# Moving the memory rows of a cross-attention into the input stage of a decoder-block kernel

## The chip, the cores and the metric

One NeuronCore of a Trainium2 chip runs the whole program. The metric is the device time of one execution in microseconds; the median of several executions counts. The engines are named as in the profile: PE (TensorE), DVE (VectorE), ACT (ScalarE), POOL (GpSimd) and SP (SyncE, which here only issues loads and stores).

## The reference, cut to what matters

One layer of a decoder: 512 tokens of width 1024, 256 memory tokens, float32.

```python
def hybrid_layer(h, mem, ...):
    z = rmsnorm(h, norm_mix) @ w_in
    z_rw, z_dsa, z_gate = _split(z, (RW_COLS, DSA_COLS, GATE_COLS))
    y_a = rwkv7_branch(z_rw, ...)          # a recurrence over the tokens, 8 heads
    y_b = dsa_branch(z_dsa, ...)           # indexer, top-k keys, attention in a latent space
    g_a, g_b = jnp.split(jax.nn.sigmoid(z_gate + b_gate), 2, axis=-1)
    h = h + (g_a * (y_a @ w_proj_a) + g_b * (y_b @ w_proj_b)) @ w_out
    h = h + cross_attention(rmsnorm(h, norm_cross), rmsnorm(mem, norm_mem), w_cq, w_ckv, w_co)
    h = h + hier_moe(rmsnorm(h, norm_ffn), ...)
    return h

def cross_attention(hn, mem_n, w_cq, w_ckv, w_co):
    k, v = jnp.split((mem_n @ w_ckv).reshape(B, M, 2, X_HEADS, X_HEAD_DIM), 2, axis=2)
    ...
```

The memory rows depend on nothing but an input: `rmsnorm(mem, norm_mem)` and its keys and values can be computed at any time before the cross-attention.

## The kernel before, in words

The kernel is written in program order and a scheduler sets each engine's instructions in an order of its own; waits follow from the places in SBUF that instructions read and write. Places are handed out by hand: `big` (object `M`) lives throughout, and further regions live for a stage. The input stage has two, `xparts` on the right of the free space (the split input rows and split weights) and `rawring` (object `E`: raw weights and scratch). When the stage is closed (`front.close()`), the regions `memory` (object `KR`) and `early` (object `MX`) are laid over them, and what is written there waits until the input stage is done with the bytes below. `memory` lies over `xparts` alone, `early` over both.

To keep float32 precision, a matrix product is made of three passes over a high and a low part. A helper (line 197, `split`) makes the parts: ACT casts the high part, DVE or POOL subtracts for the low one. `Ring.load` (line 223) loads a weight block on SP's queue and splits it; the ring's raw places and parts are reused in turn.

The stages, in the order of time:

- Input stage (to line 789). 38 blocks of `w_in`, each 24 products of line 230. The last 16 blocks are gates (lines 587 to 591): ACT takes a Tanh, POOL's queue stores the tile to DRAM. Odd gates have their low parts on POOL, even ones on DVE. Between these products runs the recurrence in 8 chunks (lines 699 to 744; the copy of line 719 and the one of line 744 are links of its chain), the group norm (lines 750 to 759, with two squares buffers `sq`), and the indexer (lines 482 to 507): scores through two buffers `rels`, then 16 pairs of a maximum (line 501) and a replacement (line 502) on DVE for each of three query tiles. The inverse of line 625 uses scratch of `E` and gives it back.
- Attention and memory stage (lines 792 to 854). `keys_values` is a generator: it normalises the memory rows (`mem_norm`, line 564: loads at 567 and 569, square at 191, root at 176, scaling at 193), transposes them (line 810), splits them into `mT`, and makes keys (line 821, 192 products of 256 columns) and values (line 832, 96 products of 512). Keys and values are stored to DRAM (lines 824, 838). `attend` (line 510) does one query tile of the sparse attention: latent queries (517), scores (524), exponential (528), transposes (537), sums (545). The scheduler sets products of line 821 between those of `attend`.
- Mixing (lines 857 to 896): both branches are lifted by `w_pa` and `w_pb` (line 887), gated and summed; the residual rows `h` are loaded from `x` (line 871). Then the output projection, the cross-attention, the router and the experts, which the change doesn't touch.

SP issues its loads in one order; one that waits holds up those behind it.

Of the kernel before, what the change touches and what calls it, by code (L numbers as in the profile page):

```python
# [13 lines left out]
T, D, P = 512, 1024, 128  # L14
NT = T // P
# [72 lines left out]
def build(tc, I, out):  # L88
    nc = tc.nc
    V, S, G, PE = nc.vector, nc.scalar, nc.gpsimd, nc.tensor  # L90
# [14 lines left out]
    M = Mem(pool.tile([P, NBIG], F32, name="big"), NBIG)  # L105

    def region(stack, name, n, dt, side=None):
        return Mem(stack.enter_context(tc.tile_pool(name=name, bufs=1, side=side)).tile([P, n], dt, name=name), n)
# [5 lines left out]
    def psum(tag="mm"):  # L114

        i = turn.get(tag, 0)
        turn[tag] = i + 1
        return PS[:, banks[tag][i % len(banks[tag])], :]
# [69 lines left out]
    def norm_tile(dst, src, gain):  # L188

        ss, rs = scr(1), scr(1)  # L190
        S.activation(dst, src, AF.Square, accum_out=ss)
        rsqrt(rs, ss, 1.0 / D, EPS)
        V.scalar_tensor_tensor(dst, src, rs, gain, op0=OP.mult, op1=OP.mult)

    def split(hi, lo, src, eng=None):

        return S.copy(hi, src).ins, (eng or V).tensor_tensor(lo, src, hi.bitcast(F32), op=OP.subtract).ins  # L197

    def split_half(hi, lo, src):

        S.activation(hi, src, AF.Copy, scale=0.5)
        V.scalar_tensor_tensor(lo, src, 0.5, hi.bitcast(F32), op0=OP.mult, op1=OP.subtract)
# [33 lines left out]
    E = region(front, "rawring", NX + NK - NR1, F32)  # L236
# [71 lines left out]
    omm = M.get(14)  # L308
# [8 lines left out]
    hb = M.get(16)  # L317
    cb = M.get(P)
    pc = M.get(4, NCH)
    msk = M.get(2, 64)  # L320
    zxg = M.get(T)
    cw = M.get(NT, 132)
    cT = M.get(T)
    zv = M.get(4, T)
    AR = M.get(4, NCH, 2, 64)
    ZV = M.get(NCH, 512)
    ST = M.get(4, NCH, 256)
    AA = M.get(4, NCH, 2, 64)
# [233 lines left out]
        yield  # L562

    def mem_norm():
        nm, raw, gm_ = MX.get(2, D), MX.get(2, D), MX.get(D)
        gmem = gm_[:, :]
        nc.sync.dma_start(gmem, I["norm_mem"].partition_broadcast(P))
        for i in range(2):
            nc.sync.dma_start(raw[:, i, :], I["mem"][i * P:(i + 1) * P, :])
        for i in range(2):  # L570
            norm_tile(nm[:, i, :], raw[:, i, :], gmem)
        raw.done()
        gm_.done()
        return nm

    def chained(*gens):
# [108 lines left out]
    gst = [E.get(T) for _ in range(2)]  # L685
    isc_ = {qt: M.get((qt + 1) * P) for qt in range(1, NT)}
    inverse()
    rels, m8s = [E.get(T) for _ in range(2)], [E.get(16, 8) for _ in range(3)]
    g2 = M.get(4 * P)
    nc.sync.dma_start(g2[:, :], I["g2"])  # L690

    St = [M.get(4, 64) for _ in range(2)]
    Sp = M.get(4, 64)
    Xs = [M.get(256) for _ in range(2)]
# [50 lines left out]


    gm, gv = M.get(NCH * 4), M.get(NCH * 4)
    sq = [M.get(2, 4, 64) for _ in range(2)]
    by_head = lambda ap: ap.rearrange("p (c a) -> p c a", a=4)
    for b in range(4):  # L750
        Yb = Ys[:, b * 2:b * 2 + 2, :].rearrange("p c (a i) -> p c a i", i=64)
# [32 lines left out]
    pace(bg, [lambda i=i: gate(i) for i in range(16)], 3)  # L784
    for _ in bg:
        pass
    for x in (hb, *gst, *rels, *m8s, omm):
        x.done()
    front.close()

# [3 lines left out]
    MX = region(early, "early", NX, F32)  # L794
# [6 lines left out]
    ringm = Ring([MX.get(512) for _ in range(4)], [KR.get(2, 512) for _ in range(2)])  # L801
    kst, vst = [MX.get(NMEM) for _ in range(2)], [MX.get(512) for _ in range(2)]

    def keys_values():
        nm = mem_norm()
        for k in range(0, KD, 2):
            pt = psum("at")
            for j in range(2):
                for i in range(2):
                    PE.transpose(pt[:, (j * 2 + i) * P:(j * 2 + i + 1) * P], nm[:, i, (k + j) * P:(k + j + 1) * P], ident)  # L810
            split(mT[:, 0, k:k + 2, :].rearrange("p a t -> p (a t)"), mT[:, 1, k:k + 2, :].rearrange("p a t -> p (a t)"),
                  pt[:, :])
        nm.done()
        yield
        for nb in range(8):
            pt = psum()
            for k4 in range(0, KD, 4):
                w = ringm.load(I["w_ck"][nb, :, k4 * P:(k4 + 4) * P], V if k4 else G)
                for a, b in ((0, 0), (0, 1), (1, 0)):
                    for k in range(4):  # L820
                        PE.matmul(pt[:, 0:NMEM], w[:, a, k * P:(k + 1) * P], mT[:, b, k4 + k, :],
                                  start=(a + b + k4 + k == 0), stop=(a == 1 and k4 + k == KD - 1))
            S.copy(kst[nb % 2][:, :], pt[:, 0:NMEM])
            nc.gpsimd.dma_start(kT_d[:, nb, :], kst[nb % 2][:, :])
            yield
        for half in range(2):
            pts = [psum(), psum()]
            for k in range(KD):
                w = ringm.load(I["w_cv"][half, k // 2, :, k % 2 * 512:k % 2 * 512 + 512], V if k % 2 else G)
                for a, b in ((0, 0), (1, 0), (0, 1)):  # L830
                    for t in range(2):
                        PE.matmul(pts[t][:, :], mT[:, a, k, t * P:(t + 1) * P], w[:, b, :], start=(a + b + k == 0),
                                  stop=(b == 1 and k == KD - 1))
                if k % 2:
                    yield
            for t in range(2):
                S.copy(vst[t][:, :], pts[t][:, :])
                nc.gpsimd.dma_start(vm_d[:, t, half * 512:half * 512 + 512], vst[t][:, :])

    kv = keys_values()  # L840
    next(kv)

# [7 lines left out]
            pass  # L850
    for _ in kv:
        pass
    for x in (St[0], St[1], Sp, *Xs, *sq, AR, ZV, ST, AA, zxg, g2, msk, pc, cw, cT, cb, *isc_.values()):
        x.done()


# [10 lines left out]
    raws = M.get(4 * D)  # L867
    ring2 = Ring([raws[:, i * D:i * D + D] for i in (1, 2, 3, 0)], [MR.get(2, D) for _ in range(3)])
    h = M.get(NT, D)
    for i in range(NT):  # L870
        nc.sync.dma_start(h[:, i, :], I["x"][i * P:(i + 1) * P, :])
    mix = M.get(KD, T)
    gts = [M.get(2, T) for _ in range(2)]
    for x, (src, wsrc) in enumerate(((yaT, I["w_pa"]), (ybT, I["w_pb"]))):
        for k in range(4):
            split(act[:, x, 0, k, :], act[:, x, 1, k, :], src[:, k, :])
        for j in range(4):
            w = ring2.load(wsrc[j])
            gt = gts[j % 2]
            nc.gpsimd.dma_start(gt.ap, gate_d[x, j])  # L880
            for n in range(2):
                nb = j * 2 + n
                pt = psum()
                for a, b in ((0, 0), (0, 1), (1, 0)):
                    for k in range(4):
                        o = (n * 4 + k) * P
                        PE.matmul(pt[:, :], w[:, a, o:o + P], act[:, x, b, k, :], start=(a + b + k == 0), stop=(a == 1 and k == 3))  # L887

                if x == 0:
                    V.scalar_tensor_tensor(mix[:, nb, :], gt[:, n, :], 1.0, pt[:, :], op0=OP.add, op1=OP.mult)  # L890
                else:
                    V.scalar_tensor_tensor(gt[:, n, :], gt[:, n, :], 1.0, pt[:, :], op0=OP.add, op1=OP.mult)
                    V.tensor_add(mix[:, nb, :], mix[:, nb, :], gt[:, n, :])
                    if nb < 4:
                        split_half(act[:, 0, 0, nb, :], act[:, 0, 1, nb, :], mix[:, nb, :])
# [691 lines left out]
```

## Time and profile before

| | us |
|---|---|
| median of 3 runs | 1287.48 |
| lowest and highest | 1281.45, 1292.67 |
| the profiled execution | 1291.4 |
| its span | 1289.6 |
| PE, DVE, ACT, POOL busy in the span | 1196.5, 642.5, 364.9, 121.9 |

The span begins with the first instruction and ends with the last; the time of an execution also holds what lies around it. A busy engine need not be at its peak: a product counts as busy until its modelled end. Times in the rows are from the span's start. "DMA to landing" is from the issue of a transfer to its completion.

### The profile page before, as it was taken

To read this page: it belongs to the slowest core of one execution; us is meant where nothing else is said; L and a number is where in the kernel's file an instruction comes from. 1 tells how busy PE (TensorE), PEld (TensorE's weight loads), DVE (VectorE), ACT (ScalarE), POOL (GpSimd) and SP (SyncE) were. 2 spreads that over 40 slices of the span, in tenths; PEclk is the share of its full clock that TensorE was granted. 3 is DMA by queue.
4 is the path that set the end of the run, shared out by engine and by line. 5 is a ranking of instruction groups with operands and counts; after the bars stand their busy time and mean duration, and the time that the engine had idled before them with its cause. 6 is when DMAs were issued, how large, how long until landed. Compare 5 with 4: busy or idle time off the path is not lost. (4 is left out here: it accounts for less than half of the span.)

```text
span 1289.6 us, 18892 instructions
## 1 busy us (share of the span) xinstructions
PE 1196.5 (93%) x7630; PEld 865.1 (67%) x7630; DVE 642.5 (50%) x1417; ACT 364.9 (28%) x666; POOL 121.9 (9%) x110
## 2 busy tenths in 40 slices
PE   5999998999993999699999989999899999999995
PEld 5867676776672878588787777654666656565662
DVE  5246688685593654366545364424333333333325
ACT  3542322334232644522445352101010101011113
POOL 1111221111130203400000020000000000000001
PEclk7989898999796999799999998999899999999998
DMA  4311113116333213474322506999699999999891
GB/s 159 98 50 34 57 57 99 43 50 238 120 115 133 70 34 109 149 260 131 131 84 84 196 34 242 421 398 421 263 421 420 420 419 421 421 421 420 357 375 66
DMA packets 52138, 272.07 MB, mean 211 GB/s; under 512 B 6064, under 2 KB 6208, under 8 KB 27728
## 3 DMA queue, kind: packets, MB, share of 16 engines
q1 hardware_dynamic: 48544, 259.21, 52.0%
q0 software_dynamic: 3504, 11.62, 2.6%
q8 instruction: 61, 1.00, 0.3%
q14 instruction: 29, 0.24, 0.1%
HBM read 261.37 MB, written 9.44 MB: 210 GB/s over the span
## 5 line engine op out<-in xcount | busy, mean ns | idle before, releaser
L230 PE MATMUL banks<-xparts 128*128 128x512 f32 x864 | 229.3, 416 | 0.5 <-DVE xparts L197 0.5
L230 PEld LDWEIGHTS banks<-xparts 128*128 128x128 f32 x864 | 166.0, 198 | 42.2 <-issue 4.5
L1443 PE MATMUL banks<-big 128*64 128x256 f32 x1616 | 180.2, 380 | 0.0
L1443 PEld LDWEIGHTS banks<-big 128*64 128x64 f32 x1616 | 116.8, 137 | 62.2 <-issue 7.8
L230 PE MATMUL banks<-weights,rounded 128*128 128x512 f32 x384 | 93.4, 396 | 0.0
L1471 PE MATMUL banks<-big 128*64 128x512 f32 x384 | 86.6, 595 | 4.6 <-DVE big L1461 2.3
L1364 DVE TENSOR_TENSOR big<-big,banks 128x512 f32<-128x512 f32 x128 | 79.4, 681 | 5.2 <-PE banks L1362 5.2
L230 PEld LDWEIGHTS banks<-weights,rounded 128*128 128x128 f32 x384 | 70.9, 188 | 14.7 <-issue 1.0
L1448 ACT ACTIVATE slot<-banks 128x256 f32<-128x256 f32 x32 | 12.3, 385 | 222.8 <-PE banks L1460 112.2
L1412 PE MATMUL banks<-chosen,rounded 128*128 128x256 f32 x512 | 69.0, 298 | 6.6 <-DVE chosen L1166 6.3
L197 ACT CAST xparts<-rawring 128x1024 fp32r<-128x1024 f32 x38 | 39.8, 1048 | 123.5 <-PE banks L230 60.8
L1412 PEld LDWEIGHTS banks<-chosen,rounded 128*128 128x128 f32 x512 | 67.1, 206 | 8.9 <-DVE chosen L1166 6.5
L1356 DVE SCALAR_TENSOR_TENSOR chosen<-banks,big,chosen 128x512 fp32r<-128x512 f32 x32 | 24.0, 750 | 87.3 <-ACT chosen L1355 87.3
L197 DVE TENSOR_TENSOR weights<-big,weights 128x1024 fp32r<-128x1024 f32 x32 | 39.0, 1223 | 53.6 <-ACT weights L197 51.3
L1362 PE MATMUL banks<-chosen 128*128 128x512 f32 x256 | 65.6, 400 | 0.0
L1471 PEld LDWEIGHTS banks<-big 128*64 128x64 f32 x384 | 27.4, 137 | 55.6 <-issue 47.4
L197 POOL TENSOR_TENSOR xparts<-rawring,xparts 128x1024 fp32r<-128x1024 f32 x20 | 48.4, 2420 | 161.0 <-ACT xparts L197 153.3
L1355 ACT ACTIVATE chosen<-banks,big 128x512 fp32r<-128x512 f32 x32 | 22.0, 688 | 137.8 <-PE banks L1471 125.9
L1428 DVE TENSOR_SCALAR chosen<-banks,big 128x512 fp32r<-128x512 f32 x16 | 12.0, 751 | 93.7 <-PE banks L1426 93.7
L197 ACT CAST weights<-big 128x1024 fp32r<-128x1024 f32 x32 | 33.5, 1052 | 80.6 <-PE banks L230 37.8
L1362 PEld LDWEIGHTS banks<-chosen 128*128 128x128 f32 x256 | 46.1, 188 | 13.4 <-DVE big L1364 2.0
L887 PE MATMUL banks<-rounded,weights 128*128 128x512 f32 x192 | 46.7, 408 | 7.5 <-ACT weights L197 7.5
(400 smaller groups left out, 1786.9 us busy)
## 6 DMA issues: line engine op xcount, KB each, us to landing
big<-in_w_e_gate SPq DMA_DIRECT2D x51, 1024.0 KB, 13.6
big<-in_w_e_up SPq DMA_DIRECT2D x50, 1024.0 KB, 13.8
big<-in_w_e_down SPq DMA_DIRECT2D x48, 1024.0 KB, 12.2
rawring<-in_w_in SPq DMA_DIRECT2D x38, 512.0 KB, 3.6
slots<-in_w_e_up SPq DMA_DIRECT2D x14, 1024.0 KB, 14.7
slots<-in_w_e_gate SPq DMA_DIRECT2D x13, 1024.0 KB, 11.5
slots<-in_w_e_down SPq DMA_DIRECT2D x12, 1024.0 KB, 11.4
big<-in_x SPq DMA_DIRECT2D x8, 512.0 KB, 5.2
```

Source lines behind the costliest of these rows:

```text
L197: return S.copy(hi, src).ins, (eng or V).tensor_tensor(lo, src, hi.bitcast(F32), op=OP.subtract).ins
L230: r = PE.matmul(pt, st(a), mv(b), start=(first and i == 0), stop=(last and i == 2))
L887: PE.matmul(pt[:, :], w[:, a, o:o + P], act[:, x, b, k, :], start=(a + b + k == 0), stop=(a == 1 and k == 3))
L1355: r = S.activation(YE[:, 0, nh, :], pd, AF.Copy, scale=g[:, :])
L1356: V.scalar_tensor_tensor(YE[:, 1, nh, :], pd, g[:, :], YE[:, 0, nh, :].bitcast(F32), op0=OP.mult, op1=OP.subtract)
L1362: PE.matmul(pc_[:, :], PT[:, t * P:(t + 1) * P], YE[:, x, nh, :], start=(x == 0), stop=(x == 1))
L1364: V.tensor_add(hh, hh, pc_[:, :])
L1412: PE.matmul(pt[:, 0:256], HL(x, t)[:, k // 4, k % 4, :], Pr_[:, t].rearrange("p e s -> p (e s)"), start=(t == 0 and x == 0), stop=(t == NT ...
L1428: V.tensor_scalar(PT[:, :], pa[:, :], slot_id[:, :], None, op0=OP.is_equal)
L1443: PE.matmul(pu[x][hf * 64:hf * 64 + 64, :], xgs[h4][:, k % 4, es_], w[:, k % 4, hf * 256:hf * 256 + 256], start=(k == 0), stop=(k == KD - 1))
L1448: S.activation(hd_[:, :], pu[0], AF.Silu)
L1471: PE.matmul(pd[j * 64:j * 64 + 64, :], ht[:, j, fb * 2 + hf, :], w[hf][j][:, fb, nh * 512:nh * 512 + 512], start=(kb == 0), stop=(kb == 3))
```

## The change

It has four edits. `mem_norm` takes its places from the input stage: the raw rows from `E` (scratch that the inverse gave back), the gain from the two `rels` buffers, which are now one place, and the normed rows from `M`. It is called before `front.close()`, so that the scheduler can set it among the input stage's work. To make room in `M`, the two squares buffers of the group norm move into the first halves of two of the four blocks of `AR`, which the recurrence reads in its first four chunks. All splits of the value weights have their low part on DVE, where every other one was on POOL. The four loads of the residual rows move from ahead of the mixing stage to behind the loads of `w_pb`.

```diff
     def mem_norm():
-        nm, raw, gm_ = MX.get(2, D), MX.get(2, D), MX.get(D)
-        gmem = gm_[:, :]
+        nm, raw = M.get(2, D), E.get(2, D)
+        gmem = rels_[:, :]
         nc.sync.dma_start(gmem, I["norm_mem"].partition_broadcast(P))
...
         raw.done()
-        gm_.done()
         return nm
...
-    rels, m8s = [E.get(T) for _ in range(2)], [E.get(16, 8) for _ in range(3)]
+    rels_ = E.get(2 * T)
+    rels, m8s = [rels_[:, i * T:i * T + T] for i in range(2)], [E.get(16, 8) for _ in range(3)]
...
-    sq = [M.get(2, 4, 64) for _ in range(2)]
+    sq = [AR[:, i].rearrange("p c x t -> p (c x t)")[:, 0:512].rearrange("p (c a i) -> p c a i", c=2, a=4) for i in range(2)]
...
-    for x in (hb, *gst, *rels, *m8s, omm):
+    nm = mem_norm()
+    for x in (hb, *gst, rels_, *m8s, omm):
         x.done()
     front.close()
...
     def keys_values():
-        nm = mem_norm()
...
-                w = ringm.load(I["w_cv"][half, k // 2, :, k % 2 * 512:k % 2 * 512 + 512], V if k % 2 else G)
+                w = ringm.load(I["w_cv"][half, k // 2, :, k % 2 * 512:k % 2 * 512 + 512], V)
...
     h = M.get(NT, D)
-    for i in range(NT):
-        nc.sync.dma_start(h[:, i, :], I["x"][i * P:(i + 1) * P, :])
...
             w = ring2.load(wsrc[j])
+            if x == 1:
+                nc.sync.dma_start(h[:, j, :], I["x"][j * P:(j + 1) * P, :])
```

On SP, the loads from the middle of the recurrence to the opening of the next stage stood so before (`in_mem` and `in_norm_mem` are the memory rows and their gain, `in_x` the residual rows, `rawring` the input stage's region, `early` the next one's):

```order
L871 DMA big<-in_x 128x1024
L223 DMA rawring<-in_w_in 128x1024 x2
L799 DMA big<-q_d 128x512
L223 DMA rawring<-in_w_in 128x1024
L799 DMA big<-q_d 128x512 x2
L223 DMA rawring<-in_w_in 128x1024
L796 DMA early<-in_w_uk 128x512
L797 DMA early<-in_w_uv 128x512
L567 DMA early<-in_norm_mem 128x1024
L569 DMA early<-in_mem 128x1024 x2
L223 DMA early<-in_w_ck 128x512 x16
```

and from the same place of the changed program on (its lines are shifted by one to seven):

```order
L878 DMA big<-in_x 128x1024
L223 DMA rawring<-in_w_in 128x1024 x2
L800 DMA big<-q_d 128x512
L223 DMA rawring<-in_w_in 128x1024
L800 DMA big<-q_d 128x512
L567 DMA rawring<-in_norm_mem 128x1024
L800 DMA big<-q_d 128x512
L223 DMA rawring<-in_w_in 128x1024
L797 DMA early<-in_w_uk 128x512
L798 DMA early<-in_w_uv 128x512
L223 DMA early<-in_w_ck 128x512 x16
```

The gain's load has moved ahead of the last two loads of the input stage; the two loads of the memory rows stand 15 rows further ahead, between loads of `w_in`, right behind the inverse; the first load of `w_ck` has none of them before it any more. The residual rows have kept their place.

On DVE, at the beginning of the indexer's last query tile, there stood the split for gate 12 (line 197) behind four maxima:

```order
L495 SCALAR_TENSOR_TENSOR big<-rawring,big 128x512 x3
L501 MAX rawring<-big 128x8
L502 MATCH_REPLACE big<-rawring,big 128x512
L501 MAX rawring<-big 128x8
L502 MATCH_REPLACE big<-rawring,big 128x512
L501 MAX rawring<-big 128x8
L502 MATCH_REPLACE big<-rawring,big 128x512
L501 MAX rawring<-big 128x8
L197 TENSOR_TENSOR xparts<-rawring,xparts 128x1024
```

and now both scalings of the memory rows (line 193) stand around it:

```order
L495 SCALAR_TENSOR_TENSOR big<-rawring,big 128x512 x3
L501 MAX rawring<-big 128x8
L502 MATCH_REPLACE big<-rawring,big 128x512
L501 MAX rawring<-big 128x8
L502 MATCH_REPLACE big<-rawring,big 128x512
L501 MAX rawring<-big 128x8
L193 SCALAR_TENSOR_TENSOR big<-rawring,big 128x1024
L502 MATCH_REPLACE big<-rawring,big 128x512
L197 TENSOR_TENSOR xparts<-rawring,xparts 128x1024
L501 MAX rawring<-big 128x8
L193 SCALAR_TENSOR_TENSOR big<-rawring,big 128x1024
```

The first scaling waits for the gain's load, which waits for the last of the three steps of line 495; the split for gate 12 stands behind it. The split for gate 14 follows five pairs later; it has moved ahead by one pair.

On PE, the end of the last query tile and the beginning of the values were

```order
L537 MATMUL banks<-big,early 128x128 x4
L821 MATMUL banks<-memory 128x256 x6
L545 MATMUL banks<-early,big 128x128 x4
L821 MATMUL banks<-memory 128x256 x8
L559 MATMUL banks<-early 64x128 x4
L821 MATMUL banks<-memory 128x256 x31
L832 MATMUL banks<-memory 128x512 x96
```

and are

```order
L537 MATMUL banks<-big,early 128x128 x4
L821 MATMUL banks<-memory 128x256 x6
L545 MATMUL banks<-early,big 128x128 x4
L821 MATMUL banks<-memory 128x256 x8
L559 MATMUL banks<-early 64x128 x4
L821 MATMUL banks<-memory 128x256 x57
L832 MATMUL banks<-memory 128x512 x96
```

so 26 more of the 192 key products come after attention. At its beginning, the 16 transposes of line 810 stand together right behind the 144 last products of line 230. On ACT, one square of the memory rows (line 191) now stands ahead of the first copy of line 719, and the other among the steps after the recurrence; each is followed by a table load for the root, and the next Tanh by another. On SP's queue one of the four loads of `w_pa` stands behind three of the residual rows.

## Rows read from the trace of the kernel before

**Rows 1.** Busy time by stretch: us, busy (instructions) per engine, PEclk, DMA share, GB/s

```profile
core 0: us, PE busy (x) PEld busy (x) DVE busy (x) ACT busy (x) POOL busy (x), PEclk, DMA share, GB/s
...
335.00:340.00 5.00, 5.00 (x18) 3.64 (x18) 0.35 (x1) 1.43 (x2) 0.00 (x0) 0.50 0.80 289
...
416.00:418.00 2.00, 2.00 (x11) 2.00 (x11) 0.68 (x2) 1.19 (x3) 0.00 (x0) 0.50 0.03 8
...
418.00:420.00 2.00, 2.00 (x16) 1.87 (x16) 1.39 (x4) 1.15 (x2) 0.00 (x0) 0.83 0.00 0
...
420.00:422.00 2.00, 1.87 (x20) 1.68 (x19) 0.81 (x3) 1.15 (x2) 0.00 (x0) 1.00 0.01 4
...
470.00:500.00 30.00, 30.00 (x206) 22.95 (x204) 18.29 (x50) 13.67 (x32) 3.12 (x4) 1.00 0.11 36
```

**Rows 2.** Time line, all engines, 370 to 425: start us, us, engine line op, count [idle before <-releaser]

```profile
397.06 0.33 SPq L796 DMA_DIRECT2D early<-in_w_uk  x1
...
406.68 1.06 ACT L191 ACTIVATE early<-early 128x1024 f32<-128x1024 f32 x1 [12.69 <-DMA early<-in_mem]
...
414.43 1.28 DVE L193 SCALAR_TENSOR_TENSOR early<-early,big 128x1024 f32<-128x1024 f32 x1
...
415.76 2.18 PE L810 MATMUL banks<-big,early 128*128 128x128 f32 x9 [2.79 <-DVE early L193]
...
419.41 1.71 PE L517 MATMUL banks<-big,early 64*128 64x128 f32 x16
...
421.26 0.49 PE L524 MATMUL banks<-big,early 128*128 128x128 f32 x2
...
422.70 1.28 ACT L528 ACT_TABLE_LOAD   x1
...
424.00 0.41 ACT L528 ACTIVATE early<-early,big 128x128 f32<-128x128 f32 x1
```

**Rows 3.** Time line of PE alone, 318 to 395

```profile
359.94 33.28 PE L230 MATMUL banks<-xparts 128*128 128x512 f32 x144
```

**Rows 4.** Time line of DVE, 330 to 385

```profile
361.60 2.45 DVE L495 SCALAR_TENSOR_TENSOR big<-rawring,big 128x512 f32<-128x512 f32 x3
...
367.49 0.69 DVE L501 MAX8 rawring<-big 128x8 f32<-128x512 f32 x1
...
369.62 1.21 DVE L197 TENSOR_TENSOR xparts<-rawring,xparts 128x1024 fp32r<-128x1024 f32 x1
...
381.24 1.21 DVE L197 TENSOR_TENSOR xparts<-rawring,xparts 128x1024 fp32r<-128x1024 f32 x1
```

**Rows 5.** Time line of ACT in the first chunk of the recurrence

```profile
235.23 0.58 ACT L668 COPY big<-banks 32x512 f32<-32x512 f32 x1 [9.86 <-PE banks L662]
...
240.99 0.37 ACT L719 COPY big<-banks 64x256 f32<-64x256 f32 x1
```

**Rows 6.** DMA issues: line, queue, op, count, KB each, median us to landing

```profile
early<-in_mem SPq DMA_DIRECT2D x2, 512.0 KB, 8.6
...
early<-in_norm_mem SPq DMA_DIRECT2D x1, 512.0 KB, 7.3
...
big<-in_norm_cross SPq DMA_DIRECT2D x1, 512.0 KB, 4.8
...
early<-in_w_uk SPq DMA_DIRECT2D x1, 256.0 KB, 2.6
```

**Rows 7.** Key and value products in the time line; then groups of the splits: busy us, mean ns

```profile
503.92 3.97 PE L821 MATMUL banks<-memory 128*128 128x256 f32 x31
...
507.73 9.82 PE L832 MATMUL banks<-memory 128*128 128x512 f32 x42
...
520.11 2.11 PE L832 MATMUL banks<-memory 128*128 128x512 f32 x6 [2.56 <-ACT memory L197]
...
L197 POOL TENSOR_TENSOR memory<-early,memory 128x512 fp32r<-128x512 f32 x16 | 21.6, 1350 | 54.9 <-ACT memory L197 48.0 <-ACT big L561 6.8
...
L197 DVE TENSOR_TENSOR memory<-early,memory 128x512 fp32r<-128x512 f32 x16 | 12.3, 768 | 27.0 <-ACT memory L197 21.9 <-PE banks L821 3.6 <-PE banks L832 1.5
```

More of the change, by code (lines that the diff above doesn't have):

```diff
@@ L852, in build @@
         pass
-    for x in (St[0], St[1], Sp, *Xs, *sq, AR, ZV, ST, AA, zxg, g2, msk, pc, cw, cT, cb, *isc_.values()):
+    for x in (St[0], St[1], Sp, *Xs, AR, ZV, ST, AA, zxg, g2, msk, pc, cw, cT, cb, *isc_.values()):
         x.done()
```

## The prediction

> **What bounds the kernel now.** I read the busy times by stretch first, because one share over the whole span hides the stages. They show TensorE (PE) busy nearly everywhere: in the middle of the attention stage it has work in 30.00 of 30.00 us [rows 1]. So work moved from one place to another is worth nothing unless it ends idle time of PE. I then looked for a hole, and the time line of all engines has one [rows 2, 3]. The last product of the input stage ends at 359.94 + 33.28 = 393.22 us. The loads for the next stage are issued only at 397.06 us, when the last gate tile has been stored and the region that held it is free. Then a chain runs with nothing beside it: the memory rows land, ScalarE (ACT) squares them at 406.68, VectorE (DVE) scales the second tile at 414.43, PE transposes at 415.76, and attention proper begins with line 517 at 419.41. That is 26 us in which PE does almost nothing, and its clock drops with it: granted 0.50 (the 1.2 GHz level) at 416 to 418 us, back to 1.00 (2.4 GHz) after 420 [rows 1]. This hole is the only stretch of such length that the change touches. Behind it PE is full again, so what is won here should arrive at the end.
>
> **The change part by part.** All of it is reckoned against the profiled execution (1291.4 us, of which 1289.6 are span).
>
> First part, memory rows. Their two loads and the load of the gain now go to the input stage's own region, so nothing of the normalisation waits for 397.06 any more. What ends the hole then? PE finishes the input stage; 397.06 - 393.22 = 3.84 us later the weights w_uk are requested, as before (the gate store is unchanged); they land 2.6 us after issue [rows 6]; then line 517 runs. The transposes of line 810 need only the normed rows and fit into these 6.4 us (16 of them; before, nine took 2.18 us [rows 2]). So with F for the end of the input stage, line 517 starts at F + 6.4 and the first scores of line 524 another 421.26 - 419.41 = 1.85 us later.
>
> Now F, which pays for the move at two places.
> (a) ACT takes a square of 1.06 us [rows 2] ahead of the copy of line 719 that ran at 240.99 us without a wait [rows 5]. That copy is a link of the first chunk of the recurrence. The memory rows must have landed by then. Their loads can go when the inverse's last products (line 662) are done, at 235.23 us [rows 5]. Landing is the open price: two loads took 8.6 us beside three others [rows 6], and a broadcast of 512 KB with less beside it took 4.8. I take 5, the nearer row, since little else is in flight; then ACT does not wait and the link is 1.1 us late, and PE has four more products of line 230 in that place (4 x 0.231 us, from 33.28 / 144) to fill it. Cost 0.5 us; bounds 0 and 3.7 (landing 8.6, so that the square ends at 245 and the link 4.6 us late, less the 0.9 of the four products).
> (b) The gain row is loaded into the buffer that the indexer's last step reads, and that step ends at 361.60 + 2.45 = 364.05 us [rows 4]. DVE's first scaling stands three steps behind it, at 367.49 + 0.69 = 368.2, and blocks DVE until the gain lands. With 4.8 us as a lower and 7.3 as an upper row [rows 6] it lands between 368.9 and 371.4; I take 5.3, 369.4, as one load of a weight block is beside it. The scaling takes 1.28 [rows 2], the split of a gate weight 1.21, and a step of the indexer 0.75 (14 of them fill the time from 370.83 to 381.24 [rows 4]): ready at 369.4 + 1.28 + 0.75 + 1.21 = 372.6 instead of 370.8. Gate 12 begins at 359.94 + 2 x 5.55 = 371.0 and needs that split in its third product, at 371.5: PE waits 1.1 to 1.2. Behind it stand one step, the second scaling and eleven steps before the split for gate 14, 12 x 0.75 + 1.28 + 1.21: ready at 384.1 instead of 382.45. Gate 14 needs it at 371.5 + 1.1 + 11.1 = 383.7; PE waits another 0.5. Cost 1.7 us; bounds 1.2 and 3.7. On SP the gain's load stands ahead of two others which wait for later events anyway.
> So F = 393.22 + 2.2 = 395.4, line 517 at 401.8, line 524 at 403.7. PE is idle for some 4 us before and the clock may have dropped; before, it came back between 2 and 4 us after PE had become dense at 415.76 [rows 1, 2], so I add 0.5: 404.2. Against 421.26 that is 17.0 us earlier.
>
> From this comes off: six products of line 821 that were done before 419.41 and must be done later, 6 x 0.128 = 0.8 (3.97 / 31 [rows 7]). Also, the new order leaves 57 of these products for the tail behind attention, where 31 stood. If PE is the limit of attention, this costs nothing; if the chain over DVE and ACT is, all 26 x 0.128 = 3.3 come on top. PE shows no idle time there, but weight loading is busy only 22.95 of 30 us [rows 1], so some of its busy time is waiting in disguise: I take 1.2. On the other side, ACT's table load before the first exponential, 1.28 us at 422.70 [rows 2], falls away because the tables for Tanh still stand; PE had products of line 821 under it, so 0.3 of its 0 to 1.3.
>
> ACT changes tables four times more in the input stage and twice less behind it. By the row one load takes 1.28 us, and the exponential starts 0.02 us after its end [rows 2]; ACT has idle time there, so the sum takes nothing beyond (a). The Trainium skill (ScalarE: Activation LUTs, "Table sets: the hidden batching unit") speaks against this: do all calls of one set before switching. The same page puts a switch at 2.66 us with a drain; by that the two switches more would cost 5.3 us if ACT were the limit, and the sum would be 10.4. The row shows no drain.
>
> Second part, the value weights. Eight splits go from GpSimd (1350 ns) to DVE (768 ns) [rows 7]. In the first seven steps PE took 9.82 / 42 = 0.234 us a product, without a wait; so the splits hide behind PE in either place. The one stall, 2.56 us before 520.11 [rows 7], waits for a weight load that queues on SP behind the load of the stored keys, and that order is unchanged. I take 0.4 us gained; bounds 0 and 2.6 (the stall goes).
>
> Third part, the residual rows. In the program's order their four loads stand where they stood, in the input stage, since their room comes free long before; one load of w_pa moves between them. All are needed 200 us later: 0. The squares of the group norm now lie in AR: they wait for half the recurrence, and the order puts them later; PE has products to run: 0, bounds -1 and 1.
>
> **Sum:** 17.0 - 0.8 - 1.2 + 0.3 + 0.4 = 15.7 us earlier: 1291.4 becomes 1275.7. The profiled execution lies 3.9 us above the median of the three timed runs, 1287.48; on that scale I predict 1271.8. About 1% (12.9 us) is what a measurement of this kernel can tell from no change.
>
> **Rivals.**
> Slow landings: the moved loads take as long as their rows of before, 8.6 and 7.3 us. For it: they now meet the w_in stream. Against: only one or two others are in flight, where five were. Then (a) costs 3.7 and (b) 3.7, 5.2 more: gain 10.5, 1277.0, within 1%.
> More than the sum: the key products and the denser start keep the clock at 1.00, and the value stage loses its stall (2.56): 15.7 + 0.5 + 2.6 - 0.4 = 18.4, 1269.1. Against it: the stalled load's place in the queue is the same.
> Slower: the clock. Attention would begin out of a sparse stretch, without the dense transposes and key products that brought the clock back at 418 [rows 1]. At 335 to 340 us PE is busy in 5.00 of 5.00 us and is granted 0.50 all the same, so being busy is not enough. At half clock a PE-bound us loses half a us; so this eats the gain when it lasts 32 us, and if it lasts through three of the four query tiles, some 60 us, it loses 30: 1287.5 - 15.7 + 30 = 1301.8. Against it: before, with products of the same kind, attention ran at 1.00. The Trainium skill (TensorE: Matmul & The Clock Gate, Part 1) calls the throttled state the default that activity releases; by that the clock would come back soon after 402, and the row at 335 to 340 shows a busy PE without it.
> The change does not do what it says: a wait on the region stays in the chain, and the hole moves at most by the mem loads' 2 us: 1285.5. Against it: the new order names the input stage's buffer as their target, and the splits of line 197 need only the weight half of that region.
>
> **How the numbers follow.** Forecast 0.50, slow landings 0.25, more 0.12, slower 0.07, not as said 0.06. The forecast's own range is 1268 to 1276, from its bounds; a tenth of it lies within 1%. So faster by over 1% has 0.45 + 0.12 = 0.57, slower by over 1% 0.07, and within 1% 0.05 + 0.25 + 0.06 = 0.36. The range runs from 1263, which is the second rival less the half of what the three timed runs differ, to 1284, which takes in the slow landings and leaves out the last two.
>
> **What would show it.** Right: line 517 about 17 us earlier, PE idle before it of 4 to 5 us instead of 26, line 810 directly behind the last product of line 230, DVE waiting for the gain's DMA near 368, and every later stage shifted by the same amount. Wrong: DVE or ACT waiting long for the memory or gain rows with PE idle before 395; a tail of line 821 that stands alone at the end of an attention stage no shorter than before; a granted clock of 0.5 beyond 410; or the same stage starts as now.

## The result and the profile after

| | before | after |
|---|---|---|
| median, us | 1288.88 (6 runs) | 1272.76 (6 runs) |
| lowest and highest | 1281.45, 1292.67 | 1269.44, 1276.07 |
| profiled execution, its span | 1291.4, 1289.6 | 1271.04, 1269.3 |
| PE, DVE, ACT, POOL busy | 1196.5, 642.5, 364.9, 121.9 | 1191.2, 646.6, 367.4, 111.9 |

The ratio is 0.9879, with a 95% interval of 0.9857 to 0.9902: 16.1 us less, between 12.6 and 18.4. The forecast was 1271.8.

The time line of the changed kernel where [rows 2 to 4] stood (columns as there; DVE and PE of the end of the input stage, then the start of attention):

```profile
356.99 0.33 SPq L567 DMA_DIRECT2D rawring<-in_norm_mem  x1
...
362.95 1.28 DVE L193 SCALAR_TENSOR_TENSOR big<-rawring,big 128x1024 f32<-128x1024 f32 x1 [1.85 <-DMA rawring<-in_norm_mem]
...
364.81 1.21 DVE L197 TENSOR_TENSOR xparts<-rawring,xparts 128x1024 fp32r<-128x1024 f32 x1
...
365.03 3.27 POOL L197 TENSOR_TENSOR xparts<-rawring,xparts 128x1024 fp32r<-128x1024 f32 x1 [4.13 <-ACT xparts L197]
...
366.08 11.17 PE L230 MATMUL banks<-xparts 128*128 128x512 f32 x48 [1.59 <-DVE xparts L197]
366.55 2.83 DVE L193 SCALAR_TENSOR_TENSOR big<-rawring,big 128x1024 f32<-128x1024 f32 x1
...
378.83 10.74 PE L230 MATMUL banks<-xparts 128*128 128x512 f32 x46 [1.57 <-DVE xparts L197]
...
389.41 1.47 PE L810 MATMUL banks<-big 128*128 128x128 f32 x12
...
393.39 0.33 SPq L797 DMA_DIRECT2D early<-in_w_uk  x1
...
396.23 3.06 PE L517 MATMUL banks<-big,early 64*128 64x128 f32 x16 [3.98 <-DMA early<-in_w_uk]
...
399.23 0.79 PE L524 MATMUL banks<-big,early 128*128 128x128 f32 x2
...
400.39 0.40 ACT L528 ACTIVATE early<-early,big 128x128 f32<-128x128 f32 x1 [0.46 <-DVE big L527]
```

The hole has closed: the last product of line 230 ends at 389.57, the transposes of line 810 follow at once, and what PE then waits for is w_uk alone, requested at 393.39. From the last product to the first score (line 524) it is 9.66 us; before it was 421.26 - 393.22 = 28.04 [rows 2, 3]. But the 144 products that ran without a gap now wait twice, 1.59 and 1.57 us, for a split on DVE. The first wait is the gain's landing with a scaling behind it: DVE begins the scaling at 362.95, and the split for gate 12 is ready at 366.02. In front of the second stands the other scaling, which took 2.83 us instead of 1.28. And the first exponential needs no table load.

The same stretches as in [rows 1], columns as there:

```profile
395.00:400.00 5.00, 3.77 (x19) 3.58 (x20) 0.00 (x0) 1.62 (x3) 0.45 (x1) 0.50 0.88 295
400.00:405.00 5.00, 5.00 (x26) 4.95 (x25) 3.40 (x14) 2.55 (x8) 1.93 (x2) 0.51 0.32 105
405.00:410.00 5.00, 5.00 (x41) 4.57 (x40) 4.03 (x19) 3.38 (x13) 0.74 (x2) 1.00 0.18 52
```

The granted clock still falls to 0.50 in the short gap, and is back at 1.00 after 405. The 16 products of line 517 took 3.06 us where they had 1.71 [rows 2].

PE at the end of attention, where [rows 7] stood:

```profile
481.02 0.66 PE L559 MATMUL banks<-early 128*64 128x128 f32 x8
481.61 7.10 PE L821 MATMUL banks<-memory 128*128 128x256 f32 x57
488.54 9.79 PE L832 MATMUL banks<-memory 128*128 128x512 f32 x42
500.15 2.70 PE L832 MATMUL banks<-memory 128*128 128x512 f32 x6 [1.82 <-ACT memory L197]
503.19 11.48 PE L832 MATMUL banks<-memory 128*128 128x512 f32 x48 [0.34 <-ACT early L837]
```

From the last product of line 559 to the first value product it is now 6.9 us, with 57 key products that stand alone; with 31 it was 3.7. The stall of the value stage is still there, 1.82 us.

### The profile page after: what moved, and what is told of

Read it like the earlier page. It is cut to its first block, busy times and chain, and to the rows that moved or that the text cites. A ratio compares the mean times of both kernels' runs of the same rounds, so it can differ in the third digit from the quotient of the medians.

```text
span 1269.3 us, 18889 instructions
## 1 busy us (share of the span) xinstructions
PE 1191.2 (94%) x7630; PEld 864.5 (68%) x7630; DVE 646.6 (51%) x1425; ACT 367.4 (29%) x668; POOL 111.9 (9%) x102
## 5 line engine op out<-in xcount | busy, mean ns | idle before, releaser
L1461 DVE COPY big<-banks 128x512 f32<-128x512 f32 x16 | 11.0, 690 | 84.1 <-PE banks L1460 84.1
```

## The experiments

Each is compared with runs of the kernel before on the same chip: the ratios are against these, with their 95% intervals. Their medians were 1288.94 us beside runs 1 to 4, 1287.17 beside 5 to 8 and 1286.12 beside 9 to 12; the changed kernel was measured once, where the kernel before had 1288.88. So medians of different sets compare to some 3 us only, and smaller steps are read from the stages. Each run has one profile, so a stage is one execution's. The stages below are read from the PE time line of each run's profile: "front" from the first product of gate 12 to the last of line 230, "start" from there to the first score, "attention" from the first score to the last product of line 559, "tail" from there to the first value product (negative where that one comes before the end of attention), "values" from the first to the last product of line 832.

| us | median | front | start | attention | tail | values |
|---|---|---|---|---|---|---|
| before | 1288.88 | 22.3 | 28.0 | 82.7 | 3.7 | 26.9 |
| changed | 1272.76 | 25.7 | 9.7 | 82.5 | 6.9 | 26.1 |
| 1 memory rows alone | 1276.49 | 28.9 | 9.7 | 82.5 | 6.9 | 26.9 |
| 2 the rest alone | 1284.30 | 22.3 | 27.3 | 82.7 | 3.7 | 26.3 |
| 3 scalings late | 1267.86 | 22.3 | 9.6 | 82.3 | 6.9 | 25.0 |
| 4 w_uk early | 1268.35 | 27.8 | 4.5 | 83.8 | 7.0 | 26.3 |
| 5 both | 1263.83 | 22.3 | 4.8 | 82.2 | 6.4 | 27.7 |
| 6 keys behind attention | 1285.78 | 25.7 | 9.6 | 85.8 | 23.1 | 25.3 |
| 7 keys paced | 1270.44 | 28.9 | 9.5 | 89.3 | -5.3 | 26.7 |
| 8 squares alone | 1285.35 | 22.3 | 28.3 | 82.7 | 3.7 | 27.1 |
| 9 before again | 1288.60 | 22.3 | 27.7 | 82.7 | 3.7 | 26.0 |
| 10 keys' load late | 1269.74 | 25.6 | 9.8 | 82.5 | 6.9 | 23.1 |
| 11 all four | 1255.65 | 22.3 | 4.8 | 87.8 | -5.3 | 26.8 |
| 12 three | 1258.28 | 22.3 | 4.8 | 82.0 | 6.4 | 23.3 |

**1 and 2: the parts.** Run 1 is the changed kernel with the value splits and the residual loads as before (those two parts of the diff undone). The squares of the group norm stay in `AR` in both runs, since the memory rows need their room.

> The changed kernel with the value weights split on both engines again and the residual rows loaded where they were. Theory A (the memory rows do it): about 1273.5 us, the changed kernel's time within its scatter; only the value stage (96 products of line 832) takes 26.9 us instead of 26.1. Theory B (5 to 7 us come out of the input stage from the other edits): 1278 us or more.

Run 2 is the complement, with the residual loads moved as in the change:

```diff
-    sq = [M.get(2, 4, 64) for _ in range(2)]
+    sq = [AR[:, i].rearrange("p c x t -> p (c x t)")[:, 0:512].rearrange("p (c a i) -> p c a i", c=2, a=4) for i in range(2)]
...
-                w = ringm.load(I["w_cv"][half, k // 2, :, k % 2 * 512:k % 2 * 512 + 512], V if k % 2 else G)
+                w = ringm.load(I["w_cv"][half, k // 2, :, k % 2 * 512:k % 2 * 512 + 512], V)
```

> The kernel before with all edits but the memory rows: value splits on VectorE, residual rows with the second branch, squares of the group norm in AR. Theory A: 1288 us, that is 0 to 1 us less than before; hole of 26 us between the last product of line 230 and line 517 as before; value stage near 26.1 us. Theory B: 1282 us, with the recurrence or what lies around it some 5 us shorter than before.

Run 1: 0.9910 (0.9875 to 0.9944), run 2: 0.9972 (0.9951 to 0.9992). So the memory rows bring most of it, but run 1 is 3.0 us slower than expected, with a front 3.2 us longer than the changed kernel's, and run 2 gained 3.6 (1.0 to 6.3) where theory A had 0 to 1. The first has a cause that the trace shows. DVE and POOL in run 1, columns as before:

```profile
365.77 1.29 DVE L193 SCALAR_TENSOR_TENSOR big<-rawring,big 128x1024 f32<-128x1024 f32 x1 [2.10 <-DMA rawring<-in_norm_mem]
...
367.58 2.33 POOL L197 TENSOR_TENSOR xparts<-rawring,xparts 128x1024 fp32r<-128x1024 f32 x1 [4.13 <-ACT xparts L197]
367.63 3.37 DVE L197 TENSOR_TENSOR xparts<-rawring,xparts 128x1024 fp32r<-128x1024 f32 x1
...
371.06 24.23 PE L230 MATMUL banks<-xparts 128*128 128x512 f32 x94 [4.01 <-DVE xparts L197]
```

The split for gate 12 takes 3.37 us on DVE instead of 1.21 [rows 4]: it began 0.05 us after POOL's split for gate 13, and ended 1.09 us after that one's end. In the changed kernel's profile DVE was first by 0.22 us; then POOL's took 3.27 us instead of 2.33, and it was the scaling behind it that took 2.83 us instead of 1.28. One order on each engine, two outcomes: one PE wait of 4.01 us (and a clock that falls behind it, front 28.9), or two of 1.6. Which one comes hangs on when the gain lands. In all six profiles with the scalings at this place POOL's split begins 1.15 us after gate 12's first product. Where the first scaling began 0.85 to 1.00 us before that product (the changed kernel, runs 6 and 10), DVE's split was first; where it began 0.21 to 0.66 us before it (runs 1, 4 and 7), POOL's was. In the kernel before, the two were 2.5 us apart [rows 4]:

```profile
372.11 2.42 POOL L197 TENSOR_TENSOR xparts<-rawring,xparts 128x1024 fp32r<-128x1024 f32 x1 [4.13 <-ACT xparts L197]
```

**3: the scalings behind the indexer.** `last[3]` is the indexer's final instruction, `behind` orders after it:

```diff
-        V.scalar_tensor_tensor(dst, src, rs, gain, op0=OP.mult, op1=OP.mult)
+        with behind(*after): V.scalar_tensor_tensor(dst, src, rs, gain, op0=OP.mult, op1=OP.mult)
...
-            norm_tile(nm[:, i, :], raw[:, i, :], gmem)
+            norm_tile(nm[:, i, :], raw[:, i, :], gmem, last[3])
```

> The changed kernel with both scalings of the memory rows behind the last step of the indexer, so that neither the gain's landing nor the scalings stand ahead of the splits for gates 12 and 14. Theory A (these two waits of 1.59 and 1.57 us cost their full length): the waits go, the 24 products of each gate run without a gap, 1269.5 us. Rival C (what is won there is lost in front of the first scores, since the transposes of line 810 become late): line 517 at the same distance of 6.7 us or more from the last product of line 230 plus the delay, 1272 to 1274 us.

PE of run 3:

```profile
355.22 33.32 PE L230 MATMUL banks<-xparts 128*128 128x512 f32 x144
388.38 0.27 PE L810 MATMUL banks<-big 128*128 128x128 f32 x1
388.87 1.42 PE L810 MATMUL banks<-big 128*128 128x128 f32 x11 [0.23 <-DVE big L193]
390.87 0.66 PE L810 MATMUL banks<-big 128*128 128x128 f32 x4 [0.57 <-DVE memory L197]
395.14 3.06 PE L517 MATMUL banks<-big,early 64*128 64x128 f32 x16 [3.62 <-DMA early<-in_w_uk]
```

The 144 products run without a gap again, as in [rows 3]; the transposes still end before w_uk lands. 0.9843 (0.9808 to 0.9878). Theory A holds: the front's 3.4 us are the price of the scalings' place. That they went through at the end at no cost is shown too (start 9.6 us, as in the changed kernel), so rival C falls.

**4 and 5: w_uk and w_uv early.**

```diff
-    wuk, wuv = MX.get(512), MX.get(512)
+    wuk, wuv = [AR[:, 2].rearrange("p c x t -> p (c x t)")[:, i * 512:i * 512 + 512] for i in range(2)]
```

> The changed kernel with w_uk and w_uv loaded into a block of AR that the recurrence has left, so that line 517 needn't wait for the input stage's region. Theory A (the hole that is left, 9.7 us from the last product of line 230 to the first score, is the wait for w_uk and its landing): line 517 directly behind the transposes, the first score 4.5 to 5.5 us behind the last product (the copy of line 519 still waits for the region), 1268.5 us. Rival D (half clock or a later wait eats it, since the next weights of line 821 still come with the region): the attention stage longer by what its start gained, 1271 to 1273 us.

PE of run 4:

```profile
394.04 1.47 PE L810 MATMUL banks<-big 128*128 128x128 f32 x12
396.23 0.66 PE L810 MATMUL banks<-big 128*128 128x128 f32 x4 [0.72 <-DVE memory L197]
396.83 1.75 PE L517 MATMUL banks<-big 64*128 64x128 f32 x16
398.67 1.37 PE L524 MATMUL banks<-big,early 128*128 128x128 f32 x6
```

Start 4.5 us, as expected, and line 517 at the full clock's 1.75 us. 0.9841 (0.9805 to 0.9877). Attention gave 1.3 back, while the clock was granted at 0.69 between 400 and 405 us; the front of this profile is the bad one with a wait of 4.01.

> The changed kernel with both edits at once: scalings behind the indexer, and w_uk and w_uv early in AR. Theory A (two separate costs): the gains of the two runs before, 4.9 and 4.4 us against the changed kernel's median, add up: 1263.5 us. Rival (the late scalings now stand in front of line 517, since nothing else holds it): line 517 some 2 us later behind the last product of line 230 than in the run with the early weights alone, 1265 to 1266 us.

Run 5: 0.9800 (0.9774 to 0.9826). Against the kernel before of its own set it is 23.3 us faster, where runs 3 and 4 have 21.1 and 20.6 and the changed kernel 16.1; so the two costs add up within the noise. The start is 4.8 us against 4.5 in run 4, so the late scalings do not stand in front of line 517 for the 2 us of the rival. The granted clock does not fall at all at the start of attention, which is back at 82.2.

**6 and 7: is attention full?** Run 6 holds every key product behind the last one of line 559 (`fin`); run 7 writes them between attention's steps.

```diff
-                        PE.matmul(pt[:, 0:NMEM], w[:, a, k * P:(k + 1) * P], mT[:, b, k4 + k, :],
+                        with behind(*fin): PE.matmul(pt[:, 0:NMEM], w[:, a, k * P:(k + 1) * P], mT[:, b, k4 + k, :],
```

```diff
-        for _ in attend(qt):
-            pass
+        for n, _ in enumerate(attend(qt)):
+            if (qt * 9 + n) % 4 == 3: next(kv, None)
```

> The changed kernel with all 192 key products (line 821) held behind the last product of attention, so that line 524 to line 559 run with nothing set between them. Theory A (attention is bound by its chain over VectorE and ScalarE, and the key products ride along): from the first score to the last product of line 559 it stays at 78 to 82.5 us, as with 135 products in it (82.45); then 192 products alone take 23.5 us, and the whole is 14 to 17 us slower than the changed kernel. Rival (TensorE is the bound there, as its busy share says): the stretch falls by 135 x 0.123 = 16.6 us to 66 us, and the whole is the changed kernel's time within 3 us.

PE of run 6, the first scores and the end of attention:

```profile
395.79 0.79 PE L524 MATMUL banks<-big,early 128*128 128x128 f32 x2
...
478.94 1.16 PE L545 MATMUL banks<-early,big 128*128 128x128 f32 x8 [0.68 <-ACT early L539]
480.88 0.66 PE L559 MATMUL banks<-early 128*64 128x128 f32 x8 [0.78 <-DVE early L548]
481.46 23.29 PE L821 MATMUL banks<-memory 128*128 128x256 f32 x192
```

Attention alone takes 85.8 us, no less than with 135 products set into it. Its clock is at half for 23.6 of them, 18 more than in the changed kernel's profile; had these cost their whole half, 9 us, 77 would be left, and still not 66. The last two query tiles settle it, since the clock stands at 1.00 there in both (the changed kernel first, then run 6; columns as in [rows 1]):

```profile
434.20:481.70 47.50, 46.73 (x314) 36.66 (x314) 27.88 (x78) 22.04 (x53) 5.60 (x7) 1.00 0.14 42
...
435.10:481.50 46.40, 39.90 (x249) 27.64 (x249) 25.94 (x76) 18.23 (x45) 1.11 (x2) 1.00 0.04 14
```

The 58 key products in the first of these stretches, 7 us of work, cost 1.1 us. This one execution is 13.0 us slower than the changed kernel's median. So a good part of TensorE's busy time in attention (30.00 of 30 us [rows 1]) is waiting in disguise: these key products ride along in a chain over PE, DVE and ACT that lasts nearly as long without them.

> The changed kernel with the key products written between the steps of attention (a group of 24 after every fourth step), so that none is left behind it. Theory A (attention has room): the tail of 57 products and 6.9 us goes, attention gets at most 2 us longer, 1267 to 1268 us. Rival (TensorE is full): attention grows by as much as the tail shrinks, 1272 to 1273 us.

0.9849 (0.9823 to 0.9874), which is neither theory's number. All 192 key products and 7 value products now lie inside, and attention is 6.8 us longer; from the first score to the end of the values it is 110.7 us instead of 115.4. Together the runs give the room: with 0, 135 and 155 key products (the last is the kernel before, 192 - 31 - 6) attention takes the same 82 to 86 us; the 37 keys and 7 values beyond 155 cost about their own time, 37 x 0.128 + 7 x 0.234 = 6.4. Whether it is their number or the even placement that costs this, no run separates.

**8 and 9: the input stage.** Run 8 is the kernel before with the first line of run 2's diff alone, run 9 the kernel before unchanged.

> The kernel before with one edit of the change alone: the two squares buffers of the group norm in AR. TensorE's order is that of the run with all edits but the memory rows. Theory E (that run's gain of 3.6 us is this edit's: it lets the scheduler set the recurrence's last chunks and the transposes behind it in another order, and the clock falls for a shorter time between 290 and 345 us): 1285 us, 3 to 4 us less than before, with 10 us at half clock between 280 and 350 us where there were 20. Rival F (the gain was scatter, or came from the value splits): 1288 to 1289 us.

> The kernel before, unchanged, for a second profile of it. Theory G (the 7 us by which gate 12 began earlier in the changed kernel's profile are mostly the clock's scatter between two executions): from the end of the inverse to gate 12 it takes 125.6 us plus half the time at half clock, as in the other profiles, and the time at half clock there differs from the 20.5 us of the first profile. Rival E (the order with the squares in AR spares it): again 17 to 21 us at half clock between 280 and 350 us, where the profiles with the squares in AR have 10 to 14.

Run 8: 0.9986 (0.9967 to 1.0004), unclear; the kernel before against itself: 1.0012 (0.9984 to 1.0041). Busy time by stretch of the first profile of the kernel before, and then of its second:

```profile
280.00:350.00 70.00, 69.49 (x427) 49.48 (x426) 42.01 (x108) 23.23 (x33) 10.07 (x9) 0.85 0.43 151
```

```profile
280.00:350.00 70.00, 69.47 (x433) 49.34 (x433) 45.89 (x110) 24.97 (x35) 10.61 (x10) 0.93 0.50 172
```

PE of the second:

```profile
353.72 33.29 PE L230 MATMUL banks<-xparts 128*128 128x512 f32 x144
```

The same program is granted 0.85 in one execution and 0.93 in another, with PE busy in both; that is some 5 us of full clock, (0.93 - 0.85) x 70, and its last 144 products begin at 353.72 instead of 359.94 [rows 3]. So theory G holds: the 7 us by which gate 12 came earlier in the changed kernel's profile can be scatter, since the unchanged kernel moved by 6.2. In the twelve profiles with the squares in `AR`, with and without the memory rows, gate 12 begins anywhere from 360.5 to 367.8 us; in these two it is 371.0 and 364.7. Run 8 by itself had come out as theory E said, 1285.35 us; E falls all the same, since the old place of the squares had the short half clock too. Whether the new order brings another 2 us, as the medians of runs 2 and 8 hint, stays open.

**10: the stall among the values.**

```diff
-    nc.sync.dma_start(kT[:, :, :], kT_d[:, :, :])
+    with behind(ringm.last): nc.sync.dma_start(kT[:, :, :], kT_d[:, :, :])
```

> The changed kernel with the load of the stored keys issued behind the last load of the value weights on SP. Theory A (the one stall of the value stage, 1.82 us here and 2.56 before, is a weight load that queues behind it): the 96 products of line 832 run without that stall, and the six behind it at full clock, 23.0 to 24.5 us instead of 26.1; 1269.5 to 1271 us. Rival (the keys then land late, and their splits wait in front of the cross-attention): the value stage shorter, what follows longer, 1272 to 1273 us.

SP of the changed kernel, then SP and PE of run 10:

```profile
482.33 9.34 SPq L223 DMA_DIRECT2D early<-in_w_cv  x7
493.70 0.33 SPq L901 DMA_DIRECT2D big<-kT_d  x1
494.12 2.77 SPq L223 DMA_DIRECT2D early<-in_w_cv  x4
...
485.10 22.40 SPq L223 DMA_DIRECT2D early<-in_w_cv  x16
507.72 0.33 SPq L901 DMA_DIRECT2D big<-kT_d  x1
...
491.29 11.16 PE L832 MATMUL banks<-memory 128*128 128x512 f32 x48
503.20 11.17 PE L832 MATMUL banks<-memory 128*128 128x512 f32 x48 [0.74 <-ACT early L837]
```

The load of the stored keys stood between the weight loads on SP's queue, and now stands behind all 16. The stall is gone and the values take 23.1 us, 3.0 less; what follows them is no longer for it, 754.1 us to the end of the span against 754.6. So the place on the queue was the cause of the stall. The times do not show the 3 us: 0.9871 (0.9845 to 0.9897) is 16.4 us less than the kernel before of this set, and the change alone had 16.1.

**11 and 12: together.** Run 12 has the edits of runs 3, 4 and 10, run 11 that of run 7 as well.

> As the run with all four edits, but without the pacing of the key products. Theory A: 1263.8 less 2 to 3: 1261 to 1262 us, with the two stalls of the value stage (0.59 and 2.40 us) gone. Rival (the stalls come from the splits, not from the queue): the value stage stays at 27 us, 1263 to 1264 us.

> The changed kernel with all four edits: scalings late, w_uk and w_uv early, key products written between the steps of attention, the load of the stored keys late. Theory A (four separate costs): 1263.8 of the run with the first two, less 2.3 for the pacing and 2 to 3 for the load: 1258.5 to 1259.5 us. Rival (with a start that is already dense the pacing only lengthens attention): 1261 to 1263 us, attention 7 us or more longer than its tail is shorter.

Run 12: 0.9781 (0.9756 to 0.9807). Run 11: 0.9758 (0.9731 to 0.9784), the best version: 30.5 us less than the kernel before of its set, where the change alone had 16.1. Both are some 3 us faster than expected, but the kernel before also has 1 us less in this set than in that of run 5, from which they were reckoned. The pacing brings 2.6 us between the two, all four executions of run 11 being faster than all four of run 12. The scatter of the input stage may have a part in it: in run 11's profile it ends 6 us earlier than in run 12's.

## Why the prediction was right, and where its terms were not

The forecast's 15.7 us less stands beside a measured 16.1 (12.6 to 18.4). By steps, each read from the profiles:

- **The hole.** Forecast from the last product to the first score: 28.0 to 8.8 with the half us for the clock, 19.2 less; measured 9.66, 18.4 less. Right: line 517 waits for w_uk, 6.66 us after the last product (forecast 6.4). The clock's half us was 1.2: 3.00 from line 517 to line 524 instead of 1.85.
- **(a), the square on ACT.** Forecast 0.5. The two rows landed in 3.9 and 5.7 us (taken: 5), ACT waited 0.35 us for the second before the square at 237.66 us, and the link came 1.3 us late (forecast 1.1). At gate 12 nothing of it is left that the scatter lets one see. The upper bound was summed wrongly: 235.23 + 8.6 + 1.06 is 244.9, so the link would be 3.9 us late and not 4.6.
- **(b), gain and scalings ahead of the gate splits.** Forecast 1.7, measured 3.4 (front 25.7 instead of 22.3), and 6.6 in the profile of run 1, outside the bounds. For gate 12 the sum held: the gain took 5.96 us from its issue to the scaling instead of 5.3, what stands behind it took 3.07 us, summed at 3.24, and PE waited 1.59 instead of 1.1 to 1.2. What failed is the step for gate 14, "12 x 0.75 + 1.28 + 1.21", forecast at 0.5 and measured at 1.57: it adds DVE's durations as if POOL were not there. The delay set DVE's work beside POOL's split for gate 13, from which its split had been 2.5 us apart, and the second scaling took 2.83 us instead of 1.28. In run 1 the same omission sits in the step for gate 12, "369.4 + 1.28 + 0.75 + 1.21", whose last term became 3.37.
- **Key products behind attention.** Forecast 0.8 + 1.2 - 0.3 = 1.7; measured 82.7 + 3.7 = 86.5 us before and 89.3 after, 2.8 lost. The mechanism was right (the chain bounds, PE's busy time holds waiting), the discount was not: 0.3 us is all by which attention became shorter with 135 products in it instead of 155. The half clock at its start hides little more: in runs 5 and 12, where it is missing, attention with 140 products takes 82.2 and 82.0 us. The 26 products more in the tail also hold the six already charged at 0.8, so the most that this step could cost was 3.3 and not 0.8 + 3.3. The prediction had listed such a tail behind an attention no shorter as a sign of being wrong; it came, and cost 1.1 us more than the sum had.
- **Value splits.** Forecast 0.4 gained. The stage takes 26.0 to 27.1 us in the four profiles with the old splits (the kernel before twice, runs 1 and 8) and 25.0 to 27.7 in six with the new (the changed kernel, runs 2 to 6), so no gain can be told; the sum below keeps the 0.4. The stall stayed, as the queue's order said.
- **Residual rows.** Forecast 0. From the last product of line 887 to the end of the span it takes 700.7 us in both profiles.

These sum to 18.4 - 3.4 - 2.8 + 0.4 = 12.6 us, and the second profile of the kernel before (span 1283.1) lies 13.8 above the changed one. So two terms were 2.8 us too cheap together, and the medians do not show it: they contain the clock's scatter, which is as large. The closeness of the hit, 15.7 to 16.1, therefore owes something to luck; 12.6 lies at the edge of the measured interval. Whether the 3.5 us between 12.6 and 16.1 are scatter or the order with the squares in `AR`, which run 2 also had (3.6, from 1.0 to 6.3), stays open.

The rivals: landings were not slow (4.8 in the median and 5.96 where 8.6 and 7.3 were the rows), so that one falls, though (b) lost 3.4 us, nearly the 3.7 that it had there, in another way. The clock came back after some 10 us, not 60. "More than the sum" did not come by itself; runs 10 and 5 show that its two ingredients, the stall and the clock at the start, were there to be had.

## What to carry to other kernels

Work moved into a full stage must be placed against what stands behind it on its own engine: two scalings of 1.28 us, set ahead of splits that had been ready less than 1 us before they were needed, cost 3.4 to 6.6, and the same two at the stage's end cost nothing. Look also at what the delayed work will then run beside on another engine. Ask of a busy TensorE what happens without the work set between; only that showed that attention had room for 155 products, while 192 made it longer. And take a second profile of the kernel before, before a few us in a stage are given a cause.

## What was not expected of the hardware

DVE and POOL held each other up. The scaling took 2.81 to 2.83 us in the three profiles where it began while POOL's split ran, 1.26 to 1.29 elsewhere, and ended about 1.1 us after POOL's end. The other way round, POOL's split took 3.17 to 3.33 us where DVE's had begun up to 0.3 us before it, and 2.33 to 2.42 elsewhere. The Trainium skill (SBUF — State Buffer, "Who interferes with whom") has it: a VectorE instruction with two SBUF inputs and a GpSimd instruction that reads SBUF share a port, and the one that comes later blocks wholly. The runs agree, either engine being the one that waited.

The granted clock in one and the same stretch differs between two executions of the same program, 0.85 and 0.93 over 70 us, while TensorE is busy in 69.5 of them in both.
